# A two-layer decoder trunk: when the second layer's key projection, decays and keys are issued, and where its last scan runs

## The chip, the cores and the metric

The kernel runs on one core of a Trainium2 chip. The metric is the device time of one execution in microseconds. TensorE (PE) multiplies, VectorE (DVE) and ScalarE (ACT) do elementwise work and empty PSUM, GpSimd (POOL) does small copies, and SyncE (SP) issues most DMAs. Each engine works through its own queue in order and waits on semaphores.

## The reference

The input x is 512 tokens by 2048 channels. Each of the two layers computes x <- x + W_out(mixer(RMSNorm(x)) * silu(gate)), in float32. The first layer is differential attention with 8 heads. The second, in which most of the change lies, is RWKV-7 time mixing with 32 heads of 64 channels:

```python
p = h @ w_in                                   # 2048 -> r, k, v, g (2048 each) and two low-rank parts
p = p + (token_shift(p) - p) * mu
r, k, v, g, dw, da = jnp.split(p, RW_SPLITS, axis=-1)
w_log = -softplus(-(w0 + tanh(dw) @ decay_up)) - 0.5
decay = exp(-exp(w_log))
a = sigmoid(a0 + da @ iclr_up)
kk = heads(k * k_k); kk = kk / max(norm(kk), 1e-12)
k = k * (1 + (a - 1) * k_a)
# per head and token: S <- S*decay + (S a_t) b_t + v_t k_t ;  y = S r_t   (a_t = -kk, b_t = kk*a)
y = group_norm(y) * gn_w + gn_b + sum(r*k*r_k) * v
out = (y * silu(g)) @ w_out
```

## The kernel before, in words

**Matmuls.** Every large product is made of three matmuls: operands are split into a high and a low half (ACT rounds, L96 and L592; DVE subtracts, L97 and L593), and `mm3` (L106) sums high·high, high·low and low·high in PSUM. One `unit_chan` (L597) is a projection of 128 channels over 512 tokens: 16 input chunks times three matmuls of 128x512, 48 in all. `unit_tok` (L145) makes 512 output columns of 512 tokens, in four token blocks: 192 matmuls. Weights come from DRAM through SP's queue (L78) into a ring of three buffers (`wraw`, 512 KB in layer 1) and are split part by part.

**The second layer.** `layer1` (L1024) walks over 16 pairs of heads (128 channels each). For pair j it projects keys K, receptances R and values V, and from pair 3 on the gate G of pair j-3 (`LAG`): the order is K R V G. Each projection is emptied by `shift_mix` (L623 on ACT, L624 on DVE: the token shift). `stage1` (L707) takes the keys and two small products of the low-rank parts and makes, on ACT and DVE:

- the decays: tanh (L719), the scan along time (L724), half of the chunk's total (L727), the subtraction (L729), exponentials (L730 to L732);
- the queries: f (L740, L743), AR (L738), l·k (L744);
- the keys: BK (L742 on ACT, L745 on DVE), the squares of the keys and their split (L747, L592, L593), and gam (L734, L735).

`stage2` (L753) puts the receptances into AR (L757) and r (L758). Behind the 18th matmul of the value projection follow `gram` (L762: all products inside the 8 chunks of 64 tokens) and `t_solve` (L814: a triangular solve in some 60 short DVE steps, L834 and L836, then L837; the result goes through DRAM by SP's queue, `td` L838 and `TT` L850, back into SBUF and is transposed on DVE, L858). `stage_v`, L881, makes the values.

**The scan.** While pair j is projected, pair j-1 goes through its 8 chunks one after another. `scan_pair` (L930) is a generator: per chunk the matmul L941 on the state VS, a copy to rhs on ACT (L944), L952 with the solved T, copies on ACT (L954), L959 and the state's update on DVE (L963 twice, L966 in chunk 0). Ahead of it `t_combine` (L844) finishes the inverse with small matmuls (L864, L874). Each `yield` gives a number of matmuls to let pass: `mm3` calls `tick` (L134) after each matmul of a projection, which counts down and issues the chain's next step behind that matmul (`issue_after`). So the order on TensorE is a comb: some matmuls of a projection, one step of the scan, and so on. `chain` (L921) takes the delay before the first step and the two gaps; they are 6 and 8 for pairs with j from 3 to 14, else 4 and 5, and 3 and 4 for the last. `others` hangs further work on a chunk: the transposes of keys (L809) on chunks 0 and 1, of values (L899) on chunk 2, and `finish_y` (L1015, with L1019 and L1021) of pair j-2 on chunk 3.

**What sets the order.** The instructions are issued under priorities: a scan step has offset `SCAN` (3000), other marked parts 2000 or 4000; those ahead in priority are placed earlier in an engine's queue. The queues are in order once built.

**Outputs.** `outputs` (L974), `centre` (L989), `group_norm` (L1001, on the tile `thg` for its squares, L1006) and `finish_y` make a pair's y. `gate` (L906) empties the gate projection, makes the tanh (L910), L911 and the product with y (L912), and stores the row to DRAM, from which `split_rows` loads it for the output projection; the last two rows stay on the chip (`split_row`, L398). After the 16 pairs the gates of pairs 13 to 15 and the last scan follow, and then the output projection in four `unit_tok` blocks, with the residual added and the result stored.

**The first layer** ends in the same way with `unit_tok`; there `all_rows` lets the last attention chain finish behind the output projection's first matmuls, by the parameter `more`.

Of the kernel before, what the change touches and what calls it, by code (L numbers as in the profile page):

```python
# [23 lines left out]
P = 128  # L24
# [89 lines left out]
class Chain:  # L114
# [30 lines left out]
def unit_tok(g, aH, aL, parts, cols, npp=NT, more=None):  # L145

    nc = g.nc
    pts = [g.pp.tile([P, 512], F32, name="pp", tag="pp") if t < npp else
           g.ps.tile([P, 512], F32, name="pt", tag="pb", bufs=2) for t in range(NT)]
    KG = 1024 // cols  # L150
    m = None
    for k0 in range(0, KT, KG):
        raw, fine = g.first.pop(0) if g.first else (None, False)
        wh, wl = split_w(g, parts, KG, cols, k0, raw, fine)
        order = [(k, t) for k in range(KG) for t in range(NT)] if fine else \
                [(k, t) for t in range(NT) for k in range(KG)]
        for i, (k, t) in enumerate(order):
            if more and i in (0, 2, 4):
                more(k0 + (k + 1 + i % 4 // 2 if fine else KG + i // 2), m)
# [267 lines left out]
def layer0(g, aps):  # L427
# [71 lines left out]
    with ExitStack() as cx:  # L499
# [24 lines left out]
        ch = Chain(g, attention(g, h, *before, 17, rows), 4)  # L524

        def all_rows(n, _):
            if n >= KT:
                ch.finish(g)

        yH, yL = Rows(rows, 0), Rows(rows, 1)  # L530
# [175 lines left out]

def stage1(g, j, k, up):  # L707

    nc, w = g.nc, g.work
    p = Pair()  # L710
    col = lambda n: g.prm[n][:, j : j + 1]
    ch = lambda ap: ap.rearrange("p (c t) -> p c t", c=NC_)
    th = []
    for i, nm in enumerate(("hw0", "ha0")):
        (uH, uL), (xH, xL) = up, g.dwda[i]
        ps = g.ps.tile([P, 512], F32, name="pt", tag="pb", bufs=2)
        mm3(nc, ps[:], uH[:, i, :], uL[:, i, :], xH[:], xL[:], True, True)
# [6 lines left out]
    nc.vector.tensor_tensor_scan(l[:].rearrange("p c t -> p (c t)"), g.rmask[:].rearrange("p c t -> p (c t)"),  # L724
                                 lw[:], 0.0, ALU.mult, ALU.add)
    m = g.small.tile([P, NC_], F32, name="m", tag="m")
    nc.vector.tensor_scalar(m[:], l[:, :, C - 1], 0.5, None, ALU.mult)  # L727
    E = w.tile([P, NC_, C + 1], F32, name="E", tag="E", bufs=1)
    nc.vector.tensor_sub(l[:], l[:], m[:, :, None].to_broadcast([P, NC_, C]))  # L729
    nc.scalar.activation(E[:, :, 0], m[:], AF.Exp, scale=-1.0)  # L730
    nc.scalar.activation(E[:, :, 1:], l[:], AF.Exp)
    nc.scalar.activation(l[:], l[:], AF.Exp, scale=-1.0)  # L732
    p.gam = g.small.tile([P, NC_], F32, name="gam", tag="gam")
    nc.vector.tensor_add(p.gam[:, 0 : NC_ - 1], m[:, 0 : NC_ - 1], m[:, 1:NC_])  # L734
    nc.scalar.activation(p.gam[:, 0 : NC_ - 1], p.gam[:, 0 : NC_ - 1], AF.Exp)  # L735
    p.AR = w.tile([P, NC_, 2, C], F32, name="AR", tag="AR", bufs=3)
    BK = w.tile([P, NC_, 2, C], F32, name="BK", tag="BK", bufs=1)
    nc.vector.scalar_tensor_tensor(p.AR[:, :, 0, :], ch(k[:]), col("nkk"), E[:, :, 0:C], ALU.mult, ALU.mult)  # L738
    f = w.tile([P, T], F32, name="f", tag="f", bufs=1)
    nc.scalar.activation(f[:], tha[:], AF.Identity, bias=col("omka"), scale=col("hka"))  # L740
    for i in range(2):
        nc.scalar.activation(BK[:, :, i, :], ch(tha[:]), AF.Identity, bias=col(f"bk_b{i}"), scale=col(f"bk_s{i}"))  # L742
    nc.vector.tensor_mul(f[:], f[:], k[:])  # L743
    nc.vector.tensor_mul(l[:], ch(k[:]), l[:])  # L744
    nc.vector.tensor_mul(BK[:], BK[:], l[:, :, None, :].to_broadcast([P, NC_, 2, C]))  # L745
    k2 = w.tile([P, T], F32, name="k2", tag="thg", bufs=1)
    nc.scalar.activation(k2[:], k[:], AF.Square, scale=col("kk"))  # L747
    p.k2 = split_act(g, k2[:], w, "x")
    p.BK, p.E, p.f = BK, E, f
# [156 lines left out]
def gate(g, j, p, gps, last=False):  # L906
# [5 lines left out]
    nc.vector.tensor_mul(gt[:], gt[:], p.y[:])  # L912
    if last:
        return split_row(g, gt[:])
    nc.scalar.dma_start(out=g.yd2[j * P : (j + 1) * P, :], in_=gt[:])


HEADS = ((0, slice(0, C)), (1, slice(C, P)))
# [11 lines left out]
def scan_pair(g, j, p, gap, gap_s, others):  # L930
# [8 lines left out]
    for c in range(NC_):  # L939
# [20 lines left out]
        for h, r_ in HEADS:  # L960
            s_ = sm[r_, o + h * C : o + h * C + C]
            if c:
                nc.vector.scalar_tensor_tensor(VS[r_, c + 1, h, :], s_, p.gam[r_, c : c + 1], Sg[r_, :],  # L963
                                               ALU.mult, ALU.add)
            else:
                nc.vector.tensor_scalar(VS[r_, c + 1, h, :], s_, p.gam[r_, c : c + 1], None, ALU.mult)  # L966
        if c in others:
# [56 lines left out]
def layer1(g, aps):  # L1024
    nc, tc = g.nc, g.tc
    with ExitStack() as cx:
# [3 lines left out]
        w = g.work  # L1030
        win = aps["rw_w_in"][0]
        pairs = []
        for j in range(D // P):
# [6 lines left out]
            def proj(i, j=j, **k):  # L1040
                return unit_chan(g, [(win, i * D + j * P, P)], P, **k)[0]

            p = stage1(g, j, shift_mix(g, proj(1), P, *mus(g, 1, j), "k", 1), up)
            r = shift_mix(g, proj(0), P, *mus(g, 0, j), "r", 1)
            pairs.append(p)
# [18 lines left out]
            vps = proj(2, behind=(18, behind))  # L1064
            stage_v(g, j, p, vps)
# [7 lines left out]
        for i in range(KT - LAG, KT - 2):  # L1073
            gate(g, i, pairs[i], proj(3, i))
        group_norm(g, j - 1, pairs[j - 1])
        finish_y(g, j - 1, pairs[j - 1])
        gps = [proj(3, i) for i in (j - 1, j)]
        rows = split_rows(g, g.yd2, ("r", "k", "th0", "th1"), 1, j - 1)
        rows.append(gate(g, j - 1, pairs[j - 1], gps[0], True))
        group_norm(g, j, p)  # L1080
        finish_y(g, j, p)
        rows.append(gate(g, j, p, gps[1], True))
        yH, yL = zip(*rows)
# [11 lines left out]
def body(ctx, tc, nc, aps):  # L1095
    g = Ctx()
    g.nc, g.tc = nc, tc
    g.last, g.first = None, []
    g.chains = []
# [39 lines left out]
```

## Time and profile before

| what | us |
|---|---|
| time before, median of 3 runs (lowest to highest) | 2250.93 (2249.58 to 2254.34) |
| the profiled execution | 2247.89 |
| its span on the core | 2246.1 |
| PE busy / PEld busy | 2185.2 / 1767.5 |
| DVE / ACT / POOL busy | 1382.1 / 1006.9 / 285.5 |

The first layer takes about the first 1035 us of the span; the sixteen pairs run from there to about 2040, and the output projection fills the rest. The profile's rows are read so: start and duration in us, engine, line, operation, output tile <- inputs, shape; in brackets the idle time ahead of an instruction and what ended it. In the rows of stretches stand the busy time and count of PE, PEld (weight loads), DVE, ACT and POOL, then the granted clock of TensorE (1.00 is full speed), the DMA share and GB/s. A row of the waits names the waiting engine and line, the one waited for, and the total in us, the times and the longest. The matmul durations in the rows are pipelined latencies; their spacing is what TensorE pays.

### The profile page before, as it was taken

The page shows a single profiled execution, that of the slowest core. Times are in us where ns is not written, and L with a number is a line of the kernel's source. Part 1 is how long each engine was busy: PE and PEld are TensorE (multiplying, and loading weights), DVE is VectorE, ACT ScalarE, POOL GpSimd, SP SyncE. Part 2 cuts the span into 40 slices and gives each one's busy share as a digit, 9 for nine tenths or more (in the row PEclk, how much of TensorE's full clock was granted, in tenths as well). Part 3 has the DMA queues.
Part 4 walks back from the last instruction along what each step waited for, and adds up shares of the span by engine and source line. Part 5 has one row for each costly group of instructions (what it writes and reads, how often), then busy time and mean ns, then how long its engine had stood idle before and what let it go on. Part 6 is the DMA issues. An engine that isn't in the chain of part 4 may idle for free. (4 is left out here: it accounts for less than half of the span.)

```text
span 2246.1 us, 33754 instructions
## 1 busy us (share of the span) xinstructions
PE 2185.2 (97%) x12260; PEld 1767.5 (79%) x12260; DVE 1382.1 (62%) x3666; ACT 1006.9 (45%) x2065; POOL 285.5 (13%) x672
## 2 busy tenths in 40 slices
PE   8999999999999999989899999999999999999999
PEld 6888888888888878877777777787777777777887
DVE  5555646455564663345677787777767787776322
ACT  4443434344343452225465555555555555555221
POOL 0000000000000000000332123232222222231000
PEclk9999999999999999999999999999999999999999
DMA  6222222232223263323422333333333333334433
GB/s 179 94 86 95 85 94 94 85 95 84 95 85 103 86 207 120 131 86 87 106 67 76 79 88 88 94 90 83 92 90 80 82 93 87 97 97 132 141 131 112
DMA packets 290730, 224.46 MB, mean 100 GB/s; under 512 B 47732, under 2 KB 255748, under 8 KB 290564
## 3 DMA queue, kind: packets, MB, share of 16 engines
q1 hardware_dynamic: 275892, 195.74, 30.0%
q0 software_dynamic: 6144, 10.84, 2.0%
q10 hardware_dynamic: 8528, 15.73, 1.9%
q8 instruction: 96, 1.57, 0.3%
q14 instruction: 70, 0.57, 0.1%
HBM read 202.26 MB, written 19.99 MB: 99 GB/s over the span
## 5 line engine op out<-in xcount | busy, mean ns | idle before, releaser
L97 DVE TENSOR_TENSOR wl<-wraw,wh 128x1024 fp32r<-128x1024 f32 (+2 forms) x325 | 395.6, 1217 | 492.8 <-ACT wh L96 488.1
L96 ACT CAST wh<-wraw 128x1024 fp32r<-128x1024 f32 (+2 forms) x325 | 340.2, 1047 | 699.8 <-PE pp L108 468.0
L108 PE MATMUL pp<-wh,hH 128*128 128x512 f32 x1408 | 554.2, 394 | 6.1 <-ACT hH L581 5.8
L108 PE MATMUL pp<-wh,hL 128*128 128x512 f32 x1408 | 552.6, 393 | 0.2 <-DVE hL L582 0.2
L108 PE MATMUL pp<-wl,hH 128*128 128x512 f32 x1408 | 552.3, 392 | 0.0
L108 PE MATMUL pp<-hL,wh 128*128 128x512 f32 (+1 forms) x1056 | 430.3, 407 | 0.1
L108 PE MATMUL pp<-hH,wl 128*128 128x512 f32 (+1 forms) x1056 | 428.8, 406 | 0.0
L108 PE MATMUL pp<-hH,wh 128*128 128x512 f32 (+1 forms) x1056 | 425.2, 403 | 2.1 <-DVE mixt L624 1.8
L108 PEld LDWEIGHTS pp<-wh,hH 128*128 128x128 f32 x1408 | 265.1, 188 | 60.2 <-ACT hH L581 6.5
L108 PEld LDWEIGHTS pp<-wh,hL 128*128 128x128 f32 x1408 | 265.1, 188 | 55.0 <-DVE hL L582 1.5
L108 PEld LDWEIGHTS pp<-wl,hH 128*128 128x128 f32 x1408 | 265.2, 188 | 52.6 <-DVE wl L97 0.3
L108 PEld LDWEIGHTS pp<-hH,wh 128*128 128x128 f32 (+1 forms) x1056 | 199.2, 189 | 40.6 <-DVE mixt L624 2.2
L108 PEld LDWEIGHTS pp<-hL,wh 128*128 128x128 f32 (+1 forms) x1056 | 199.5, 189 | 37.3 <-DVE hL L582 1.7
L108 PEld LDWEIGHTS pp<-hH,wl 128*128 128x128 f32 (+1 forms) x1056 | 199.6, 189 | 33.2
L834 DVE SCALAR_TENSOR_TENSOR tmpl<-LT,Tm 128x60 f32<-128x60 f32 (+24 forms) x496 | 133.2, 269 | 12.6
L947 POOL COPY SA<-VS 64x64 f32<-64x64 f32 x224 | 59.2, 264 | 445.3 <-DVE VS L963 402.5
L836 DVE TENSOR_TENSOR Tm<-Tm,tmpl 128x60 f32<-128x60 f32 (+24 forms) x496 | 105.1, 212 | 11.5 <-DVE tmpl L834 0.4
L673 POOL MEMSET rmask<- 128x512 bf16 x1 | 0.5, 524 | 833.7 <-DVE nb L334 833.7
L963 DVE SCALAR_TENSOR_TENSOR VS<-sm,gam,Sg 64x64 f32<-64x64 f32 x192 | 54.3, 283 | 52.7 <-PE sm L959 48.6
L944 ACT COPY rhs<-sm 64x64 f32<-64x64 f32 x256 | 52.5, 205 | 72.8 <-PE sm L941 70.1
L941 PEld LDWEIGHTS sm<-VS,G 128*128 128x128 f32 x256 | 43.4, 188 | 43.1 <-issue 29.5
L954 ACT COPY VS<-sm 64x64 f32<-64x64 f32 x256 | 52.6, 206 | 53.4 <-PE sm L952 48.7
(269 smaller groups left out, 2813.2 us busy)
## 6 DMA issues: line engine op xcount, KB each, us to landing
wraw<-in_rw_w_in_dram SPq DMA_DIRECT2D x128, 512.0 KB, 4.0
wraw<-in_da_w_in_dram SPq DMA_DIRECT2D x254, 256.0 KB, 3.0
wraw<-in_da_w_out_dram SPq DMA_DIRECT2D x32, 512.0 KB, 3.6
wraw<-in_rw_w_out_dram SPq DMA_DIRECT2D x32, 512.0 KB, 3.6
LT<-ltd POOLq DMA_DIRECT2D x64, 132.0 KB, 2.9
yr<-yd SPq DMA_DIRECT2D x28, 256.0 KB, 3.9
xq<-in_x_dram SPq DMA_DIRECT2D x16, 256.0 KB, 4.9
xd<-xq ACTq DMA_DIRECT2D x16, 256.0 KB, 3.4
```

What stands on the lines that cost most here:

```text
L96: nc.scalar.copy(hi[:, ks], raw[:, ks])
L97: nc.vector.tensor_sub(lo[:, ks], raw[:, ks], hi[:, ks].bitcast(F32))
L108: m = nc.tensor.matmul(out, a, b, start=s, stop=e)
L673: nc.gpsimd.memset(g.rmask[:], 1.0)
L834: nc.vector.scalar_tensor_tensor(tt, LT[:, i : i + 1, i + 1 :].to_broadcast([P, s, n]), n2[:, i : i + 1], Tm[:, 0:s, i : i + 1].to_broadca ...
L836: nc.vector.tensor_add(Tm[:, 0:s, i + 1 :], Tm[:, 0:s, i + 1 :], tt)
L941: nc.tensor.matmul(sm[:, 0:P], both(p.G[:, c, 0]), both(VS[:, c]), start=True, stop=True)
L944: nc.scalar.copy(rhs[r_, :], sm[r_, h * C : h * C + C])
L947: nc.gpsimd.tensor_copy(p.SA[r_, c - 1, :], VS[r_, c, h, :])
L954: nc.scalar.copy(VS[r_, c, h, :], sm[r_, P : P + C])
L963: nc.vector.scalar_tensor_tensor(VS[r_, c + 1, h, :], s_, p.gam[r_, c : c + 1], Sg[r_, :], ALU.mult, ALU.add)
```

## The change

In the second layer:

- The key projection and `stage1` of pair j+1 are issued before the gate projection of pair j-3, its receptance projection after it. The projections so go V, K of the next pair, G, R of the next pair.
- `stage1` ends behind tanh and the decay's bias. The rest becomes three functions, `decays`, `queries` and `keys`, which are put in a list `g.later`; `Chain.step` takes one from the list behind each scan step that has issued a state update (L963 of after's `scan_pair` notes it in `g.state`), with `issue_after` on that update. `stage2` issues what is left. L734 and L735 (gam) go to the end of `keys`; f (L740) goes to the decays, BK's L742 to the queries.
- `gate` is cut in two: `gate` makes gt with the tanh, `gated` the product with y and the store.
- The gaps of the scan of pair 0 are 3 and 4, it begins 28 matmuls later, and the gram of pair 1 no longer issues a step of pair 0's chain right behind itself (`before`).
- The last pair's chain has delay 80 and gaps 4 and 4. It is finished inside the output projection's first block, by `all_rows`, when the last input chunk comes up; then its group norm, `finish_y` and `gated` follow. The gate of pair 15 is projected and its tanh made before.
- `unit_tok`, in both layers, goes chunk by chunk (k outside, token block inside) in the last part of a block if it was given `more`; in the first layer the last row is awaited at `n >= KT - 1` instead of `KT`.

The diff, cut to its core:

```diff
 class Chain:
     def step(self, g):
         with g.tc.high_priority(offset=SCAN):
             self.wait = next(self.steps, None)
+        if g.state and g.later:
+            with g.tc.issue_after(g.state.ins):
+                g.later.pop(0)()
+        g.state = None
...
 def unit_tok(...):
-        order = [(k, t) for k in range(KG) for t in range(NT)] if fine else \
+        by_k = fine or more and k0 + KG == KT
+        order = [(k, t) for k in range(KG) for t in range(NT)] if by_k else \
...
 def stage1(g, j, k, up):
+    def decays():
+        nc.vector.tensor_tensor_scan(l...)            # L724
+        nc.vector.tensor_scalar(m...)                 # L727
+        nc.vector.tensor_sub(l...)                    # L729
+        nc.scalar.activation(p.E[:, :, 0]...); nc.scalar.activation(p.E[:, :, 1:]...)
+        nc.scalar.activation(l...)
+        nc.scalar.activation(p.f...)
+    def queries():
+        nc.vector.tensor_mul(p.f...)                  # L743
+        nc.vector.scalar_tensor_tensor(p.AR...)       # L738
+        nc.vector.tensor_mul(l...)                    # L744
+        for i in range(2):
+            nc.scalar.activation(p.BK[:, :, i, :]...) # L742
+    def keys():
+        nc.vector.tensor_mul(p.BK...)                 # L745
+        nc.scalar.activation(k2...)                   # L747
+        p.k2 = split_act(g, k2[:], w, "x")
+        nc.vector.tensor_add(p.gam...)                # L734
+        nc.scalar.activation(p.gam...)
+    g.later += [decays, queries, keys]
...
 def stage2(g, j, r, p):
+    while g.later:
+        g.later.pop(0)()
...
 def layer1(g, aps):
+        begin(0)
+        r = receptances(0)
         for j in range(D // P):
...
-                chain(g, j - 1, pairs[j - 1], 5, 6 if full else 4, 8 if full else 5, others).step(g)
+                gaps = (6, 8) if full else (4, 5) if j > 1 else (3, 4)
+                chain(g, j - 1, pairs[j - 1], 5, *gaps, others).step(g)
+                if j == 1:
+                    pairs[0].chain.wait += 28
...
-                    gram(g, j, p, j and pairs[j - 1].chain)
+                    gram(g, j, p, j > 1 and pairs[j - 1].chain)
...
+            if j + 1 < D // P:
+                begin(j + 1)
             if j >= LAG:
-                gate(g, j - LAG, pairs[j - LAG], proj(3, j - LAG))
-        chain(g, j, p, 5, 3, 4)
+                gated(g, j - LAG, pairs[j - LAG], gate(g, j - LAG, proj(3, j - LAG)))
+            if j + 1 < D // P:
+                r = receptances(j + 1)
+        chain(g, j, p, 80, 4, 4)
...
+        def all_rows(n, _):
+            if n >= KT and len(rows) < KT:
+                group_norm(g, j, p)
+                finish_y(g, j, p)
+                rows.append(gated(g, j, p, gt, True))
...
-            pts = unit_tok(g, yH, yL, [(aps["rw_w_out"][0], cb * 512, 512)], 512, 2)
+            pts = unit_tok(g, yH, yL, [(aps["rw_w_out"][0], cb * 512, 512)], 512, 2, more=all_rows)
```

More of the change, by code (lines that the diff above doesn't have):

```diff
@@ L158, in unit_tok @@
             if more and i in (0, 2, 4):
-                more(k0 + (k + 1 + i % 4 // 2 if fine else KG + i // 2), m)
+                more(k0 + (k + 1 + i % 4 // 2 if by_k else KG + i // 2), m)
             kk = k0 + k
@@ L526, in all_rows @@
         def all_rows(n, _):
-            if n >= KT:
+            if n >= KT - 1:
                 ch.finish(g)
@@ L738, in stage1 @@
[L738 to L745, printed above, removed]
@@ L903, in turn_values, with gate @@
             nc.scalar.copy(p.VS[(1 - h) * C : (2 - h) * C, par : NC_ : 2, h, :], pv[par * C : par * C + C, :, h, :])
-def gate(g, j, p, gps, last=False):
+def gate(g, j, gps):
     nc, w = g.nc, g.work
@@ L911, in gate, with gated @@
     nc.vector.scalar_tensor_tensor(gt[:], th[:], 1.0, gt[:], ALU.add, ALU.mult)
-    nc.vector.tensor_mul(gt[:], gt[:], p.y[:])
+    return gt
+def gated(g, j, p, gt, last=False):
+    g.nc.vector.tensor_mul(gt[:], gt[:], p.y[:])
     if last:
         return split_row(g, gt[:])
-    nc.scalar.dma_start(out=g.yd2[j * P : (j + 1) * P, :], in_=gt[:])
+    g.nc.scalar.dma_start(out=g.yd2[j * P : (j + 1) * P, :], in_=gt[:])
 HEADS = ((0, slice(0, C)), (1, slice(C, P)))
@@ L962, in scan_pair @@
             if c:
-                nc.vector.scalar_tensor_tensor(VS[r_, c + 1, h, :], s_, p.gam[r_, c : c + 1], Sg[r_, :],
-                                               ALU.mult, ALU.add)
+                g.state = nc.vector.scalar_tensor_tensor(VS[r_, c + 1, h, :], s_, p.gam[r_, c : c + 1], Sg[r_, :],
+                                                         ALU.mult, ALU.add)
             else:
@@ L1032, in layer1, with proj, begin @@
         pairs = []
-        for j in range(D // P):
+        def proj(i, j, **k):
+            return unit_chan(g, [(win, i * D + j * P, P)], P, **k)[0]
+        def begin(j):
             c0 = j * P
@@ L1038, in layer1, with receptances @@
             up = split_act(g, u[:], w, "up")
[L1040 to L1045, printed above, removed]
+            pairs.append(stage1(g, j, shift_mix(g, proj(1, j), P, *mus(g, 1, j), "k", 1), up))
+        def receptances(j):
+            return shift_mix(g, proj(0, j), P, *mus(g, 0, j), "r", 1)
+        begin(0)
+        r = receptances(0)
+        for j in range(D // P):
+            p = pairs[j]
             if j:
@@ L1069, in layer1 @@
                 turn_values(g, p)
+            if j + 1 < D // P:
+                begin(j + 1)
             if j >= LAG:
[L1071 to L1074 removed]
+                gated(g, j - LAG, pairs[j - LAG], gate(g, j - LAG, proj(3, j - LAG)))
+            if j + 1 < D // P:
+                r = receptances(j + 1)
+        chain(g, j, p, 80, 4, 4)
+        gated(g, j - 2, pairs[j - 2], gate(g, j - 2, proj(3, j - 2)))
+        gps = proj(3, j - 1)
         group_norm(g, j - 1, pairs[j - 1])
         finish_y(g, j - 1, pairs[j - 1])
[L1077 to L1083, printed above, removed]
+        row = gated(g, j - 1, pairs[j - 1], gate(g, j - 1, gps), True)
+        gt = gate(g, j, proj(3, j))
+        rows = split_rows(g, g.yd2, ("r", "k", "th0", "th1"), 1, j - 1) + [row]
+        def all_rows(n, _):
[3 more added lines that the diff above has]
+                rows.append(gated(g, j, p, gt, True))
+        yH, yL = Rows(rows, 0), Rows(rows, 1)
         for cb in range(4):
             cs = slice(cb * 512, (cb + 1) * 512)
[L1086 removed]
+            pts = unit_tok(g, yH, yL, [(aps["rw_w_out"][0], cb * 512, 512)], 512, 2, more=all_rows)
             for t in range(NT):
@@ L1098, in body @@
     g.last, g.first = None, []
-    g.chains = []
+    g.chains, g.later, g.state = [], [], None
     g.const = ctx.enter_context(tc.tile_pool(name="const", bufs=1))
```

39 lines of the change are left out of this document (22 added, 17 removed).

## The prediction

> **What bounds the kernel now.** I read the page's first table, then the waits of PE, then the order of DVE in front of the wait that recurs. The page:
>
> ```profile
> span 2246.1 us, 33754 instructions
> PE 2185.2 (97%) x12260; PEld 1767.5 (79%) x12260; DVE 1382.1 (62%) x3666; ACT 1006.9 (45%) x2065; POOL 285.5 (13%) x672
> ```
>
> TensorE is the bound, and the change takes no matmul away. All that can be won is time in which TensorE waits or issues late. For layer 1 (1035 us to the end) the waits of PE are, in us in total, times, longest:
>
> ```profile
> PE sm L941 <- DVE VS L963: 14.8, 14, 1.2
> PE px L864 <- DVE T L858: 6.4, 3, 4.4
> PE sm L941 <- DVE VS L966: 2.9, 1, 2.9
> PE sm L952 <- ACT rhs L944: 1.4, 3, 0.8
> ```
>
> The first row is one wait of about 1.17 us in each of twelve pairs. One of them, and a matmul row further on that fixes the true period of a 128x512 matmul (12 in 2.72 us, so 0.227 each; the 0.39 in the rows is a pipelined latency):
>
> ```profile
> 1521.30 0.39 PE L108 MATMUL pp<-hH,wh 128*128 128x512 f32 x1
> 1522.86 0.46 PE L941 MATMUL sm<-VS,G 128*128 128x128 f32 x2 [1.17 <-DVE VS L963]
> 2095.35 2.72 PE pp L108 x12
> 1473.80:1536.50 62.70, 61.27 (x422) 49.30 (x420) 48.27 (x130) 34.85 (x79) 17.32 (x41) 1.00 0.34 89
> ```
>
> The scan's next step was issued 1.56 us after the matmul before it, where 0.227 would do: the wait costs 1.33 us of a 62.70 us pair (last row: the stretch of one pair, with busy PE, PEld, DVE, ACT, POOL). What makes the state late stands in the order of DVE. The state update of chunk 2 ends at 1497.10, and from there to the update of chunk 6 DVE has no idle time:
>
> ```profile
> 1496.81 0.29 DVE L963 SCALAR_TENSOR_TENSOR VS<-sm,gam,Sg 64x64 f32<-64x64 f32 x1
> 1519.25 1.22 DVE L724 TENSOR_TENSOR_SCAN l<-rmask,th 128x512 f32<-128x512 bf16 x1
> 1520.59 0.68 DVE L743 TENSOR_TENSOR f<-f,mixk 128x512 f32<-128x512 f32 x1
> 1521.29 0.68 DVE L729 TENSOR_TENSOR l<-l,m 128x512 f32<-128x512 f32 x1
> 1522.42 0.29 DVE L963 SCALAR_TENSOR_TENSOR VS<-sm,gam,Sg 64x64 f32<-64x64 f32 x1
> ```
>
> The decay scan and two more row-wide operations stand directly ahead of chunk 6's update, which ends at 1522.71; TensorE follows at 1522.86. I call 1497.10 A: before, the four next steps' L941 start at A+6.77, 12.16, 18.95 and 25.75, and without any wait the last would be at A+24.42.
>
> **The change, part by part.**
>
> *Steady pairs.* The order of after's DVE queue puts the decays (L724, L727, L729) behind chunk 3's update, the queries (L743, L738, L744) behind chunk 4's, the keys (L745, L593, L734) behind chunk 5's. DVE stays without a gap, so what counts is the sum in front of chunk 6's update. These enter that stretch (the scan, l and f were in it already):
>
> ```profile
> 1523.03 0.74 DVE L738 SCALAR_TENSOR_TENSOR AR<-mixk,prm_nkk,E 128x512 f32<-128x512 f32 x1
> 1524.23 0.69 DVE L744 TENSOR_TENSOR l<-mixk,l 128x512 f32<-128x512 f32 x1
> 1524.95 1.23 DVE L745 TENSOR_TENSOR BK<-BK,l 128x1024 f32<-128x1024 f32 x1
> 1527.23 0.68 DVE L593 TENSOR_TENSOR sLx<-k,sHx 128x512 fp32r<-128x512 f32 x1
> ```
>
> With starts 0.08 us before the end shown for the operation in front, and 0.13 for L734, that is +3.1 us. Behind the update go the value mixes L911 and L912 (0.6 each, -1.2) and nine small steps of the triangular solve (L834, L836; -2.2 at their present spacing). That alone is only -0.3. The rest is spacing:
>
> ```profile
> 1510.23 1.22 DVE L97 TENSOR_TENSOR wl<-wraw,wh 128x1024 fp32r<-128x1024 f32 x1
> 1511.37 0.23 DVE L836 TENSOR_TENSOR Tm<-Tm,tmpl 128x70 f32<-128x70 f32 x1
> 1513.11 0.23 DVE L836 TENSOR_TENSOR Tm<-Tm,tmpl 128x66 f32<-128x66 f32 x1
> 1513.37 0.28 DVE L834 SCALAR_TENSOR_TENSOR tmpl<-LT,Tm 128x60 f32<-128x60 f32 x1
> ```
>
> An independent neighbour starts 0.08 us before the end shown (10.23 + 1.22 against 11.37), a dependent one 0.03 us after it (13.11 + 0.23 against 13.37). In after's order some eight more of the solve's steps have an independent operation between them, 0.11 each: -0.9. So chunk 6's update ends at about A+24.5, not 25.6. Going through the steps the same way, L941 comes at A+8.2, 13.8, 19.5 and 24.75, with two waits of about 0.4 left: a gain of 1.0 per pair. At most it is 1.33, at least 0 (all of it lost to the next point). I charge 0.1 for a second limit: ACT now has the casts, tanh, decay, f and both BK activations ahead of chunk 4's rhs copies, in one run. The nearest row, of the 62.7 us from 1485.8:
>
> ```profile
> L742 ACT ACTIVATE BK<-th,prm_bk_b,prm_bk_s 128x512 f32<-128x512 f32 x2 | 1.6, 812 | 0.0
> ```
>
> If both stand uncovered ahead of the copies this is 1.6 us; I count the copies 0.3 late, in a step where DVE is late by more. Twelve waits are shown, the first belongs to the start-up: 11 x 0.9 = **-10 us** (bounds -14.6 and +3.3, that is 1.33 won or 0.3 net lost per pair).
>
> The solve pays for it: its last step moves from A+27.2 to about A+29.7. What follows it:
>
> ```profile
> 1523.89 0.43 DVE L837 TENSOR_TENSOR Tm<-Tm,LT 128x256 f32<-128x256 f32 x1
> 1524.39 0.37 SPq L838 DMA_DIRECT2D td<-Tm  x1
> 1530.31 0.44 DVE L858 STREAM_TRANSPOSE T<-TT 64x256 f32<-64x256 f32 x1
> 1535.50 1.09 PE L864 MATMUL px<-T,G 32*32 32x32 f32 x32
> ```
>
> From the end of L837 to the second L858 pass 6.0 us, and L864 then waits 4.8 us in the queue for its turn (A+38.4). In after the data are there at A+35.7 and L864's turn is at A+37.4. In DVE's order L858 now stands around the eviction of the receptance projection and L757, which puts the second L858's end at about A+37.4 too: cover just enough. SP's queue is moved as well: td now stands behind two weight loads, the second of which needs a buffer that comes free at about A+29.4. I charge nothing; if the cover is gone, the wait is at L864 (rival 2).
>
> *Start-up (pairs 0 to 3).* The scan of pair 0 has few matmuls between its steps. Two successive starts, and the stretch from chunk 1 to chunk 4 (PE, PEld, DVE, ACT, POOL, then clock):
>
> ```profile
> 1132.31 0.46 PE L941 MATMUL sm<-VS,G 128*128 128x128 f32 x2
> 1135.87 0.46 PE L941 MATMUL sm<-VS,G 128*128 128x128 f32 x2
> 1128.70:1139.39 10.69, 10.22 (x47) 6.37 (x46) 8.31 (x32) 5.21 (x18) 3.60 (x10) 1.00 0.20 51
> 1226.75 0.69 PE L864 MATMUL px<-T,G 32*32 32x32 f32 x16 [1.69 <-DVE T L858]
> 1227.60:1231.00 3.40, 3.40 (x23) 2.36 (x22) 1.89 (x4) 1.50 (x3) 3.35 (x4) 0.50 0.58 164
> 1271.70:1275.10 3.40, 3.35 (x16) 2.62 (x16) 3.33 (x8) 3.27 (x9) 0.24 (x1) 1.00 0.24 38
> 1678.10:1681.50 3.40, 3.40 (x10) 2.75 (x10) 3.20 (x8) 1.29 (x2) 0.99 (x4) 0.50 0.37 109
> ```
>
> A step takes 3.56 us. Of the 47 matmuls in three steps 29 are full-width, 29 x 0.227 = 6.6, and 18 are the scan's at some 0.1: 8.4 of 10.69 us, so 0.75 us is lost per step, the round through ACT, PE and DVE. In after's order the scan of pair 0 starts 26 matmuls later behind the gram, has ten to twelve instead of nine matmuls per step and ends six matmuls ahead of the next gram instead of thirty. Each added matmul fills 0.227 us: with two to three more per step, 0.5 x 7 steps = 3.5, and 0.9 off the 4.4 us wait for T (four matmuls' worth more cover): -4.5. The gram of pair 1 no longer issues a step of that chain right behind itself; the number of matmuls stays the same. For pair 1 the same filling (some 2 us) is lost again, as its T solve has less cover and its L864 waits about 1.3 longer: 0. For pair 2, the wait of 1.69 us is followed by 3.4 us at a granted clock of 0.50, which costs 1.7; both go if its solve, started some 4 us earlier, is in time: -3.4. The 1.17 wait at 1271 shrinks by 0.5. Together **-8.5 us**; bounds -12 and -2, since none of these rows shows the new order. What tells when a wait costs double is the clock column: 0.50 behind 1.69 us, 1.00 behind 1.18 us.
>
> [...]
>
> *Tail.* The last scan now runs inside the first block of the output projection, not beside the last two gate projections:
>
> ```profile
> 2042.58:2074.17 31.59, 30.09 (x153) 20.55 (x154) 18.94 (x35) 19.34 (x53) 10.63 (x20) 1.00 0.54 167
> PE sm L952 <- ACT rhs L944: 0.8, 1, 0.8
> PE pt L1019 <- DVE yc L1012: 0.6, 1, 0.6
> ```
>
> 153 matmuls in 31.59 us: 78 full-width (17.7 us) and 75 of the scan, some 8.3 with their switching, leave 5.6 us lost, the 0.8 wait among it; the 0.6 at L1019 stands just before. With gaps of 4 for 3 and the scan over about 100 matmuls I take two thirds back, 3.9, and the 0.6: **-4.5 us** (bounds -6 and -2). The row that this scan gives is first needed for the last input chunk, now the 180th of 192 matmuls since the last part goes chunk by chunk (by_k); its transposes (L1019) come as the 156th, 24 x 0.227 = 5.4 us ahead, against some 3.5 us for L1021, L912 and the two halves of split_row. Evictions of the four blocks end within the last twelve matmuls instead of spread out; four additions of 0.7 us fit.
>
> *Layer 0.* by_k in its last part and a later finish of its last attention chain change no matmul and no count; what ends there last, TensorE's wait for the norm, stays: 0, within 0.3.
>
> **Sum.** -8.5 - 10 - 4.5 = -23. The profiled execution took 2247.89 us (span 2246.1 and 1.8 around it), so 2224.9; the median of the runs shown is 2250.93, 3.0 above it. I forecast that median: **2228 us**.
>
> **Rivals.**
>
> *1. The steady gain does not come (about 2237).* DVE has no idle time from chunk 2 to chunk 6 either way; without the spacing gain the sum falls by 0.3 only, and if ACT is late as well the wait moves to chunks 4 and 5. Then only start-up and tail pay: 2250.9 - 13 = 2238, less a little. For it: ACT's long run in front of the copies. Against it: the two spacings in the rows. [...] The rows show a start before the shown end for independent neighbours, and so speak for a gain.
>
> *2. Slower (about 2270): T comes too late in each pair.* Place: SP's queue, td behind two weight loads, and L858, with L757 queued behind it on DVE and the gram behind that. One load in the way:
>
> ```profile
> wraw<-in_rw_w_in_dram SPq DMA_DIRECT2D x128, 512.0 KB, 4.0
> ```
>
> T then lands up to 4 us later, L864 waits 2 to 3 us, and above 1.69 us of idle the half clock adds 1.7: about 4 a pair, 3 net of the gain, 11 x 3 = +33 against the other -13: +20. It decides from 1.7 us of delay on, as there is no slack beyond A+37.4. Against it: the buffer that the load waits for comes free before the solve's end, and issuing takes 0.4 us, not 4.
>
> *3. Nothing net (about 2250).* Small waits at L864 (0.3 to 0.9 per pair) and ACT's lateness use up the 0.9 per pair, and the start-up's tighter solves bring half clocks of their own that cost what its scans win.
>
> **Chances.** Forecast 0.56 (own range 2219 to 2234), rival 1 0.20, rival 3 0.10, rival 2 0.14. All lower bounds together, -12 - 14.6 - 6 = -32.6, give 2218; all upper ones, -2 + 3.3 - 2, give 2250. Range 2217 to 2252, which leaves out rival 2 and a little. 0.2% is 4.5 us, about what a measurement of this kernel can tell from no change: faster 0.76, same 0.10, slower 0.14.
>
> **What would show it.** In the changed profile: waits of L941 for L963 in the steady pairs two of about 0.4 us or none, a pair of 61.7 to 61.9 us between grams, no wait of L864 for T beyond pair 2, and no clock of 0.50 after 1300 us but for the single 2.9 us wait at L966 (the clock row at 1678; a one-off, in no sum). The gram of pair 2 about 4.5 us earlier; the scan in the output projection with steps of 3.5 us or more and no wait at L1019. The forecast is wrong if L864 shows a wait in each pair, if L952 waits for ACT's copies in each pair, or if the solve's late end pushes DVE's work past the gram.

## The result and the profile after

The changed kernel takes **2236.76 us** (median of 4 runs, 2235.41 to 2238.46) against 2250.26 us (4 runs, 2249.11 to 2254.34). The ratio is 0.9937, with a 95% interval of 0.992 to 0.9954: faster by 13.5 us. I had forecast 2228 us, 23 us faster, in a range from 2217 to 2252 (2219 to 2234 for the forecast proper).

The first lines of the page of the changed kernel:

```profile
span 2233.7 us, 33774 instructions
PE 2184.1 (98%) x12260; PEld 1770.4 (79%) x12260; DVE 1374.9 (62%) x3666; ACT 1005.1 (45%) x2065; POOL 297.4 (13%) x672
```

The span is 12.4 us shorter and TensorE's busy time nearly the same: only waiting went. The starts of the sixteen grams (the first L773 of before, L789 of after) cut both traces into stretches with the same matmuls, so the difference can be located (one profile of each kernel):

| stretch | before, us | after, us | measured | forecast |
|---|---|---|---|---|
| start to gram of pair 1 | 1102.45 | 1102.19 | -0.3 | 0 |
| pair 1 to pair 2 | 60.03 | 61.30 | +1.3 | -4.5 |
| pair 2 to pair 4 | 122.92 | 117.96 | -5.0 | -4.0 |
| pair 4 to pair 15 (eleven pairs) | 694.73 | 691.32 | -3.4 | -10 |
| pair 15 to the end | 265.97 | 260.93 | -5.0 | -4.5 |

Two stretches fell short, the eleven steady pairs and the one from pair 1 to pair 2. The waits of PE in the eleven pairs of after:

```profile
PE px L880 <- DVE T L874: 3.7, 8, 0.8
PE sm L961 <- DVE VS L986: 2.9, 1, 2.9
PE sm L979 <- ACT VS L974: 2.5, 11, 0.2
PE sm L961 <- DVE VS L983: 2.0, 11, 0.2
PE gp L789 <- DVE AR L773: 0.8, 1, 0.8
```

The wait of 1.17 us for the state is gone from each pair; a fifth of a microsecond is left in two places. In the first row stands what took its place: L880 (L864 of before) waits for T in some of the pairs; before has no such wait in these eleven. The lone 2.9 us came back at the same pair, so it is no one-off, as I had called it; it belongs to both kernels.

In a pair that lost nothing, DVE's order in after, from chunk 2's update (first row) to chunk 6's (last but one), and TensorE's step behind it:

```profile
1489.91 0.29 DVE L983 SCALAR_TENSOR_TENSOR VS<-sm,gam,Sg 64x64 f32<-64x64 f32 x1
1499.89 1.22 DVE L738 TENSOR_TENSOR_SCAN l<-rmask,th 128x512 f32<-128x512 bf16 x1
1503.90 0.29 DVE L983 SCALAR_TENSOR_TENSOR VS<-sm,gam,Sg 64x64 f32<-64x64 f32 x1
1506.58 0.74 DVE L749 SCALAR_TENSOR_TENSOR AR<-mixk,prm_nkk,E 128x512 f32<-128x512 f32 x1
1509.61 0.29 DVE L983 SCALAR_TENSOR_TENSOR VS<-sm,gam,Sg 64x64 f32<-64x64 f32 x1
1510.06 1.28 DVE L756 TENSOR_TENSOR BK<-BK,l 128x1024 f32<-128x1024 f32 x1
1514.98 0.29 DVE L983 SCALAR_TENSOR_TENSOR VS<-sm,gam,Sg 64x64 f32<-64x64 f32 x1
1515.43 0.46 PE L961 MATMUL sm<-VS,G 128*128 128x128 f32 x2
```

The scan, AR and BK each have an update behind them, and L961 follows chunk 6's update without a wait. Half of what the pair wins stands elsewhere, though, where no wait was shown. The scan's first matmul on rhs in a pair, in before and in after:

```profile
1481.05 0.43 PE L952 MATMUL sm<-rhs,TT 128*128 128x64 f32 x2
1474.42 0.33 PE L972 MATMUL sm<-rhs,TT 128*128 128x64 f32 x2
```

The full-width matmul ahead of the first row starts at 1480.51, 0.54 us earlier; the one ahead of the second at 1474.18, 0.24 us earlier. With a like 0.17 us at the next chunk, chunk 2's update comes 22.7 us behind the gram instead of 23.3. Now the pair that ends at 1592.41: first SP's queue with two weight loads, then td and TT; then DVE and TensorE.

```profile
1579.21 3.38 SPq L78 DMA_DIRECT2D wraw<-in_rw_w_in_dram  x2
1582.68 0.53 SPq L854 DMA_DIRECT2D td<-Tm  x1
1588.48 1.82 SPq L866 DMA_DIRECT2D TT<-td  x4
```

```profile
1590.23 0.44 DVE L874 STREAM_TRANSPOSE T<-TT 64x256 f32<-64x256 f32 x1 [1.61 <-DMA TT<-td]
```

```profile
1590.73 0.69 PE L880 MATMUL px<-T,G 32*32 32x32 f32 x16 [0.81 <-DVE T L874]
1591.80 0.69 PE L880 MATMUL px<-T,G 32*32 32x32 f32 x16 [0.39 <-DVE T L874]
```

The TT loads wait for td to land, 5.8 us after its issue; in before 1524.39 to 1526.73, 2.3 us, was usual (eight of the eleven pairs; 2.9 to 4.0 in the others). In after td takes 4.2 to 5.8 us in ten of them, in the clean pair too. The second load of the first row is issued at 1582.2, half a microsecond ahead of td. DVE stood idle for 1.6 us for the data, and TensorE 0.8 and 0.4 us behind it (the second since L773 stands between the two transposes on DVE). Stretches of a clean pair, of this one, and of the gram that follows it (the third column from the right is the granted clock):

```profile
1467.49:1529.16 61.67, 61.19 (x424) 49.31 (x421) 47.60 (x131) 34.47 (x79) 18.57 (x41) 1.00 0.35 90
1529.16:1592.41 63.25, 61.54 (x423) 49.33 (x420) 47.66 (x131) 34.91 (x79) 18.57 (x41) 1.00 0.35 88
1592.40:1595.80 3.40, 3.40 (x35) 3.39 (x32) 0.13 (x1) 2.42 (x5) 0.00 (x0) 0.51 0.40 119
```

The clean pair takes 61.67 us, 1.04 less than before, as forecast. The late one takes 63.25, and the gram behind it runs at half clock for 3.4 us, which costs the next pair 1.7 more (63.40 us). Behind a like wait, 0.82 and 0.44 us at 1784, the clock stayed at 1.00.

### The profile page after: what moved, and what is told of

It is laid out like the page before. It is cut to its first block, busy times and chain, and to the rows that moved or that the text cites. A ratio compares the mean times of both kernels' runs of the same rounds, so it can differ in the third digit from the quotient of the medians.

```text
span 2233.7 us, 33774 instructions
## 1 busy us (share of the span) xinstructions
PE 2184.1 (98%) x12260; PEld 1770.4 (79%) x12260; DVE 1374.9 (62%) x3666; ACT 1005.1 (45%) x2065; POOL 297.4 (13%) x672
## 5 line engine op out<-in xcount | busy, mean ns | idle before, releaser
L970 POOL TENSOR_SCALAR Sg<-SA,gam 128x64 f32<-128x64 f32 x96 | 72.1, 751 | 9.3
```

Of the source, the lines that this page charges most:

```text
L970: nc.gpsimd.tensor_scalar(Sg[:], p.SA[:, c - 1, :], p.gam[:, c : c + 1], None, ALU.mult)
```

## The experiments

Theory: in the steady pairs the load on SP right ahead of td makes T late; the gain of 1.0 us per pair is there and is given back at L880. Rivals: T is late because the solve ends 2.5 us later on DVE, whatever SP does; or the gain itself is missing in part.

**The load behind TT.** Only the second half of the key weights moves, from pair 4 on. They are loaded two pairs ahead, so the edit acts on T of pair 2 and of those after it.

```diff
+        after = g.last or k0 and g.hold
-        with g.tc.issue_after(g.last) if g.last else ExitStack():
+        with g.tc.issue_after(after) if after else ExitStack():
             ld = g.nc.sync.dma_start(...)
...
+    g.tdq = m.ins                    # the last TT load
...
+            g.hold = g.tdq if j > 3 else None
+            ps = proj(1, j)
+            g.hold = None
```

> The changed kernel with one edit: from pair 4 on, the second half of the key projection's weights (512 KB) is issued on SP behind the four TT loads instead of right ahead of td. Theory (the load in front of td on SP's queue delays T): TT's issue comes 2.3 to 3 us after the solve's end instead of 4.4 to 6.0, no wait of L880 for T in the steady pairs, no clock of 0.5 at their grams, all steady pairs at 61.7 to 61.9 us; 7 us less, 2229 to 2231 us. Rival A (T is late because the solve ends later, the load is harmless): TT's issue stays at 4.4 us or more, 2236 to 2238 us. Rival B (the load is only put off and comes too late for its own cast): waits of L108 for wl, 2237 us or more.

Measured: 2230.2 us (2225.68 to 2231.67), ratio to before 0.9916 (0.9901 to 0.9931). SP's queue at the pair that ends at 1528.99, and its L882 (L880 of after):

```profile
1520.72 0.38 SPq L855 DMA_DIRECT2D td<-Tm  x1
1523.06 1.82 SPq L867 DMA_DIRECT2D TT<-td  x4
1524.93 1.85 SPq L79 DMA_DIRECT2D wraw<-in_rw_w_in_dram  x2
```

```profile
1527.97 1.09 PE L882 MATMUL px<-T,G 32*32 32x32 f32 x32
```

td lands in 2.3 us again, the load comes behind TT, and L882 has no wait. The waits of PE in its eleven pairs hold no row for T any more:

```profile
PE sm L963 <- DVE VS L988: 2.8, 1, 2.8
PE sm L981 <- ACT VS L976: 2.6, 12, 0.2
PE sm L963 <- DVE VS L985: 1.9, 11, 0.2
```

Over the pairs TT's issue comes 2.4 to 3.5 us after the solve's end (after: 4.4 to 6.0, and 3.1 in the last), all but the long pair take 61.5 to 62.1 us, and the eleven pairs 685.6 us, 9.1 less than before and 5.7 less than after. The solve ends as late as in after (53.1 to 53.5 us behind the gram in the ordinary pairs of both). So the load was the cause, and the rival with the solve's end falls.

**The load between td and TT.** The same edit, with td in place of the last TT load (`g.prev` is td of the pair whose T is on its way).

```diff
+    g.tdq = nc.sync.dma_start(out=g.td[...], in_=Tm[:]).ins
...
+            g.hold = g.prev if j > 3 else None
```

> The changed kernel with the same load issued between td and the TT loads. If the order in the queue decides (td is served after what was issued ahead of it), td lands in about 2.4 us again, but the TT loads now come behind the 512 KB: their landing takes 3 to 4 us instead of 1.8, and the sum of both is 1 to 2 us better than in the changed kernel: 2231 to 2235 us. If the transfers only share the engines, whatever their order, td still takes 4 us or more: 2236 to 2238 us.

Measured: 2239.09 us (2237.45 to 2241.06), ratio 0.9959 (0.9945 to 0.9973): not faster than after (the intervals overlap), against the first reading. SP's queue at one pair, the landing of its TT loads, and the waits for T in all of layer 1 (in after 7.1 us, 12 times):

```profile
1780.29 0.38 SPq L855 DMA_DIRECT2D td<-Tm  x1
1780.76 0.53 SPq L79 DMA_DIRECT2D wraw<-in_rw_w_in_dram  x1
1782.83 2.10 SPq L867 DMA_DIRECT2D TT<-td  x4
```

```profile
DMA to landing us min/median/max: 2.4/3.4/3.6
```

```profile
PE px L881 <- DVE T L875: 8.4, 9, 2.8
```

This is the worst of the steady pairs. Over the ten that the edit reaches, td, now ahead of the load, lands in 2.3 to 3.6 us instead of 4.2 to 5.8, and the slowest of the TT loads behind it in 2.0 to 3.6 us instead of 1.9 to 2.2. The eleven pairs take 688.1 us, 3.2 less than in after and 2.5 more than with the load behind TT. So in this run the order decides, and there the first reading held. The total did not follow, for a place that neither reading had looked at, the solve of pair 2, where two weight loads come between td and TT:

```profile
1221.86 1.12 SPq L79 DMA_DIRECT2D wraw<-in_rw_w_in_dram  x2
1229.32 0.69 PE L881 MATMUL px<-T,G 32*32 32x32 f32 x16 [2.43 <-DVE T L875]
1230.80:1241.04 10.24, 10.24 (x68) 7.85 (x67) 5.56 (x17) 5.05 (x12) 2.15 (x5) 0.50 0.40 106
```

The TT loads land there in 4.7 to 5.0 us instead of 2.0 to 2.3, L881 waits 2.4 us instead of 0.7, and half clock follows for 10.2 us (last row) where after has none: pair 3 to pair 4 takes 70.4 us instead of 65.4. Another 2.6 us of this profile stand ahead of the gram of pair 1, where the edit has no part. In these runs, then, what is issued shortly behind a 512 KB load lands late (td in 4.2 to 5.8 us instead of 2.3, TT in up to 3.6 instead of 2.2), and the load costs least behind the whole round trip (685.6 us for the eleven pairs, against 688.1 and 691.3).

**The parts at once.**

```diff
-    g.later += [decays, queries, keys]
+    for part in decays, queries, keys:
+        part()
```

> The changed kernel with decays, queries and keys issued at once at the end of stage 1 instead of in parts behind three state updates. Theory (the parts win, since the 3.1 us of queries and keys otherwise stand ahead of chunk 4's update, with waits of DVE for ACT's exponentials between them): L961 waits 1.5 to 4 us in each steady pair, half clock behind it where it is above 1.7 us; pairs of 63.5 to 66 us, 2255 to 2285 us. Rival (the key projection ahead of the gate does it alone): pairs as in the changed kernel, 2235 to 2239 us.

Measured: 2242.44 us (2238.77 to 2243.48), ratio 0.997 (0.996 to 0.998). Six of its eleven steady pairs take 62.6 to 62.7 us, the others 61.6 to 64.2 and the long one 66.8: between the two expectations, and for another reason than mine. The waits of PE from 1470 to 1660 us hold one row, and none for the state:

```profile
PE sm L980 <- ACT VS L975: 0.7, 3, 0.2
```

The wait for the state is gone without the parts (in all eleven pairs but the long one): with the keys emptied right behind chunk 3, the queue's own order already has the scan ahead of chunk 4's update and AR and BK ahead of chunk 5's. That pairs are no shorter comes from elsewhere: the two halves of L881 now stand around and inside the gram.

```profile
1659.32 0.69 PE L881 MATMUL px<-T,G 32*32 32x32 f32 x16
1659.93 0.48 PE L790 MATMUL gp<-AR,BK 64*128 64x128 f32 x2
1660.35 0.69 PE L881 MATMUL px<-T,G 32*32 32x32 f32 x16
```

Adding up the starts on TensorE, L881, gram and L891 take 0.5 to 0.7 us longer in such a pair than in after's clean pair and the scan's steps 0.4. So the key projection's place removes the wait, but no time: the eleven pairs take 695.0 us, against 694.7 in before and 691.3 in after. The 1.0 us per pair came only with the parts in their fixed places, and not for my reason: without them L881 and the scan's steps lose as much as the wait cost.

**The start-up as before.**

```diff
-                gaps = (6, 8) if full else (4, 5) if j > 1 else (3, 4)
+                gaps = (6, 8) if full else (4, 5)
-                if j == 1:
-                    pairs[0].chain.wait += 28
-                    gram(g, j, p, j > 1 and pairs[j - 1].chain)
+                    gram(g, j, p, j and pairs[j - 1].chain)
```

> The changed kernel without its start-up edits: pair 0's gaps are 4 and 5, no 28 matmuls of delay, the gram of pair 1 issues a step of its chain. Theory (the edits lose 1.3 us between the grams of pairs 1 and 2 by a longer stretch at half clock, and win 2.5 us in each of the next two): 60 us between grams 1 and 2, 55 and 67 us in the next two; 3 to 4 us more, 2240 to 2241 us. Rival (the 2.5 us of the two later stretches come from the order of the projections and the parts, not from these edits): 60, 52.6 and 65.4 us; 1 us less, 2235 to 2236 us.

Measured: 2240.06 us (2232.98 to 2246.82), ratio 0.9958 (0.9942 to 0.9974). Its runs spread over 14 us, so the total does not tell it from after; the one profile does, stretch by stretch. Pair 1 to 2 takes 61.05 us, 2 to 3 54.22, 3 to 4 66.52. The three stretches sum to 181.8 us against 179.3 in after and 183.0 in before. So the edits bring 2.8 us behind pair 2, and the rest there, 2.2, comes from the rest of the change. That the edits lengthen the first stretch, as I had it, is not so: it hardly changes without them, though half clock lasted some 7 us here and 10 in after.

**Both kernels, profiled a second time.**

> The kernel before, unchanged, profiled a second time: what repeats between two profiles. If the length of the half clock behind pair 0's wait belongs to the kernel, it is again 3.4 us, and grams 1 to 2 are 60.0 us apart; if it belongs to the moment at which the wait falls, it may be 3.4 or 6.8 us and the stretch differs by up to 2 us. td to TT 2.3 to 4.1 us and steady pairs of 62.7 us either way, and the long pair of 67 us at 1662 again.

> The changed kernel, unchanged, profiled a second time. Theory: TT's issue again 4.4 to 6.0 us after the solve's end in every steady pair, and the sum of the eleven pairs within 2 us of 691.3, though the pairs that lose need not be the same ones, since T misses L880's turn by tenths of a microsecond. If the losses belonged to certain pairs, the same ones lose again. Half clock behind pair 0's wait again about 10 us.

Measured: 2249.39 and 2235.85 us. First the stretch from pair 1 to pair 2 in before, its repeat, after and its repeat:

```profile
1102.45:1162.48 60.03, 54.80 (x369) 40.35 (x369) 43.07 (x129) 30.24 (x73) 19.13 (x41) 0.97 0.29 71
```

```profile
1102.72:1162.99 60.27, 55.38 (x368) 40.75 (x368) 43.04 (x129) 30.31 (x73) 18.80 (x41) 0.94 0.28 72
```

```profile
1102.19:1163.49 61.30, 57.69 (x369) 42.45 (x369) 44.19 (x132) 30.72 (x73) 18.95 (x41) 0.92 0.31 77
```

```profile
1105.33:1165.39 60.06, 56.13 (x368) 41.36 (x369) 44.14 (x132) 30.76 (x73) 18.98 (x41) 0.94 0.32 78
```

The clock's mean of 0.97, 0.94, 0.92 and 0.94 says 3.4, 6.8, 10.2 and 6.8 us at half speed: (1 - 0.94) x 60 / 0.5 is about 7. The time at half speed is here one, two or three pieces of 3.4 us, and not the same in two profiles of one kernel. With equal clocks (the two repeats) the stretch is 60.27 against 60.06: the change wins 0.2 us there, one profile each. The +1.3 of the first comparison so goes with the clock, though a piece has no fixed price here: one more cost before 0.24 us (60.03 to 60.27) and after 1.24 (60.06 to 61.30). The kernel with the old start-up, also at some 7 us, took 61.05: read so, the edits win 1.0 us, and the rest of the change costs 0.8. In the first profiles of both kernels the stretches at half clock begin whole numbers of 3.413 us apart, in before at 1118.3, 1227.6 and 1678.1 (32 and 132 such pieces) and in after at 1118.0, 1592.4 and 1670.9 (139 and 23). So where a wait falls on this grid of 3.413 us may matter, an estimate of mine from two places in after: both waits at 1592 lie in the piece from 1589.0 to 1592.4, with 1.20 us of idle, and half clock follows; at 1784, with the clock at 1.00 behind it, a border at 1783.6 (56 pieces behind 1592.4) parts the idle into 0.45 and 0.81. The idle in a piece alone does not decide: 1.06 us, all in the piece that begins at 1101.3, was not enough in before, while waits of 0.37 and 0.36 us were in after's repeat (below).

In before again the steady pairs take 62.7 us and the long one 66.9. In after's repeat TT's issue came 4.3 to 5.9 us after the solve's end (2.8 in the last pair), and the eleven pairs take 689.2 us, 2.2 less than in the first profile. Four pairs lost in both: those that end at 1407, 1594, 1658 and 1787 us took 62.5, 63.3, 64.2 and 63.2 (1405, 1592, 1656 and 1786 us in the first: 62.4, 63.3, 63.4, 63.2). Two more lost in the first only, those that end at 1910 and 1973 (62.7 each; 61.6 and 62.0 in the repeat). What singles the four out stays open. Half clock came again behind the waits at 1592 (0.79 and 0.36 us here), and here also behind 0.37 and 0.36 us at 1658, for 6.8 us.

**Pair 0's scan 50 matmuls later,** on the kernel with the load behind TT.

```diff
-                gaps = (6, 8) if full else (4, 5) if j > 1 else (3, 4)
+                gaps = (6, 8) if full else (4, 5) if j > 1 else (2, 3)
-                    pairs[0].chain.wait += 28
+                    pairs[0].chain.wait += 50
```

> The kernel with the key load behind TT, and pair 0's scan 50 instead of 28 matmuls later with gaps of 2 and 3: L880 of pair 0 then stands behind 52 instead of 42 matmuls. Theory (the 2.3 us wait and the 10 us of half clock behind it cost 2.3 + 5 us between grams 1 and 2, the scan's shorter gaps 2 to 3): no wait above 1 us, no half clock, grams 1 to 2 at 55.5 to 57 us, total 2225 to 2227 us. Rival (the clock falls for another reason, or the scan with 2 and 3 matmuls between its steps loses as much): 60 us or more, 2229 to 2232 us.

Measured: 2232.45 us (2231.21 to 2234.41), ratio 0.9921 (0.9906 to 0.9936); pair 1 to 2 takes 60.38 us. This did not test the theory, as the edit made a wait of its own:

```profile
PE px L882 <- DVE y L906: 4.6, 1, 4.6
```

So late in the order, the tile of L882's products shares its PSUM buffer with the one from which L906 makes y, and has to wait for it.

**The end as before.**

```diff
-        chain(g, j, p, 80, 4, 4)
+        chain(g, j, p, 5, 3, 4)
...
-            pts = unit_tok(..., 512, 2, more=all_rows)
+            pts = unit_tok(..., 512, 2)
```

(with group norm, `finish_y` and `gated` of the last pair ahead of the output projection again)

> The changed kernel with the end of before: the last pair's chain with delay 5 and gaps 3 and 4 beside the last two gate projections, its row made before the output projection, no chunk-by-chunk order there. Theory (the scan's place is worth what the traces differ by, 5.1 us): 266 us from the last gram to the end instead of 260.9, total 2241 to 2243 us. Rival (the end is shorter for another reason, for instance since gates and loads no longer meet): 261 to 263 us, 2236 to 2239 us.

Measured: 2240.66 us (2236.74 to 2243.37), ratio 0.9953 (0.994 to 0.9966). From the last gram to the end it takes 265.79 us, against 260.93 in after and 265.97 in before, and the two waits of before are back:

```profile
PE sm L972 <- ACT rhs L964: 0.9, 1, 0.9
PE pt L1039 <- DVE yc L1032: 0.6, 1, 0.6
```

The scan's place is worth 4.9 us; only the total came a little under the expected one.

**One comparison on one chip.** The changed kernel, the load behind TT from pair 4 on, and from pair 2 on (`if j > 1`).

> The changed kernel again, on one chip with the next two, so that the edit's worth is read from one comparison. About 0.6% under before, 2235 to 2238 us; the pairs that end at 1405, 1592, 1656 and 1786 us lose again.

> The kernel with the key load behind TT again, in five rounds. Theory: about 7 us under the changed kernel on the same chip, 2228 to 2231 us, 0.85 to 0.95% under before, with an interval that does not reach the changed kernel's ratio. If the first comparison was luck of the chip, within 3 us of the changed kernel.

> The same edit for the pairs 2 and 3 as well, which moves a few instructions of the start-up. If T's lateness costs there too (0.7 us of wait at pair 2), 1 us less than the version with pair 4 on; if the start-up is bound by its clock and its scan, no difference, and up to 2 us more where the scan's place moves.

Measured against one before of 2249.01 us: 2234.86 us (ratio 0.9935, 0.9923 to 0.9947), 2231.03 us (0.9918, 0.9905 to 0.9931) and **2227.8 us** (0.9911, 0.9896 to 0.9925). The edit is worth 3.8 us there between the medians. The interval of the second does reach the first kernel's ratio, against what I expected; the traces carry the verdict: 692.0 us for the eleven pairs, 684.2 and 684.5, some of it the clock's, as half clock took 10.2 us of these pairs in the first, none in the second and 3.4 in the third. Over all the profiles taken, after needs 691.3, 689.2 and 692.0 us for them and the kernels with the load behind TT 685.6, 685.8, 684.2 and 684.5: some 6 us less on average. In after's profile here the pairs that end at 1406, 1592, 1658 and 1787 lost again (62.5, 63.3, 65.7, 62.4). The third version is 3.2 us below the second, but their intervals overlap. Its profile gains 2.3 us, nearly all in the first stretch (58.62 us from pair 1 to 2 against 60.91). There the edit also moves a load that stood between td and TT of pair 0: the wait for T is 1.7 us instead of 2.2, and half clock lasts 6.8 us instead of 10.2. After's repeat, with as much half clock, took 60.06.

## Why the prediction was right, and where it was short

- **The number: in the wide range, outside the narrow one.** 2236.76 us lies within 2217 to 2252, which adds all bounds up, but not within 2219 to 2234, where I had the forecast at 0.56. It lies beside rival 1's 2237, and that is chance: rival 1 let DVE keep the state late, but the state came on time, and most of the gain was lost at T.
- **Steady pairs, the wait removed: right, the size partly by luck.** 62.71 to 61.67 us in a clean pair; I had 1.0 before a charge of 0.1. L961 stands 8.2, 14.1, 19.9 and 25.2 us behind chunk 2's update, 0.0 to 0.5 later than I had it. So from there the last step comes only 0.5 us earlier than before (25.75), not 1.0; the other 0.6 was won ahead of chunk 2's update, where I had counted nothing. The two small waits left are shown as 0.2 and cost 0.4 and 0.3 in spacing, as I had them; but 24.42 without any wait and two of 0.4 make 25.2, so my 24.75 did not follow from my own waits. Without the late T the eleven pairs win 9.1 us (load behind TT); I had 10. That the parts were needed is right for the time and not for the wait: the key projection's place alone removes the wait and wins nothing.
- **"I charge nothing" for T's way: the step that failed.** I let 6.0 us pass from the solve's end to the start of the second L858, as in before (where it is 6.0 to 7.3). Measured: 7.3 to 8.9 us in after, since td's landing took 4.2 to 5.8 us (2.9 in the last pair) instead of 2.3. I had seen the two loads ahead of td in the queue, but counted only the time at which the second is issued, not that td's transfer runs behind its 512 KB. L880 waited in the pairs with 5 us and more, 0.4 to 1.3 us, and half clock added 1.7 behind one of them. That is rival 2, in place and mechanism, at a fraction of its size: of the 11 us that eleven clean pairs would win, 7.6 are missing, 0.7 per pair instead of 4. The waits shown for T (3.7 us), that half clock (1.7) and one wait for AR (0.8, at the last pair) make 6.2 of them; with the load behind TT 5.7 came back.
- **"above 1.69 us of idle the half clock adds": too lax.** Two waits of 0.81 and 0.39 with small matmuls between them were enough (the clock row of 0.51 above), and so were 0.37 and 0.36 in the repeat; 0.82 and 0.44 at another pair were not.
- **Start-up, pair 1 to 2: wrong.** I had -4.5, it is about -0.2 at an equal clock. The wait for T did shrink (4.1 to 2.6 us between the repeats), but the filling did not save the scan's steps: summed over the stretch, the first matmuls of the steps start some 2.8 us later than the spacing of full-width matmuls (0.227 us) would have it, in both repeats. The updates and copies come later too, as DVE and ACT now hold the next pair's keys in that stretch. That last sentence is argued from the order, not tried.
- **Start-up, pair 2 to 4: -5.0, forecast -4.0,** but otherwise divided: -2.5 and -2.5 where I had 0 and -4. Without the start-up edits it is -2.2.
- **Tail: right.** -5.0 against -4.5, and undone by itself +4.9. No wait at L1039, none at the scan.
- **Layer 0: not resolved.** -0.3 in the first profiles, +2.6 in the repeats, where after had half clock for 3.4 us at 1037.8; other profiles of after's start-up lie between.
- **Sum.** -23 forecast, -12.4 measured in the spans and -13.5 in the medians. In the spans 6.6 are missing in the steady pairs and 5.8 in the first stretch; pair 2 to 4, the tail and layer 0 gave 1.8 more.

## What to carry to other kernels

When a change uses up slack, look at what stands ahead of each small transfer in its queue: here a 512 KB load half a microsecond ahead of a 128 KB store added 2 to 3.5 us to its landing, and one edit of the order brought some 6 us in eleven pairs. Such an edit must be followed through every place that it reaches: with the load between td and TT the steady pairs won 3.2 us, and the stretch behind pair 2's solve lost 5, half clock included. That a wait is gone does not mean that its time is won: with the parts issued at once the wait was gone and the pairs took as long as before. And a stretch that ends in a short idle of TensorE should be profiled twice, since the time at half clock was not the same in two profiles here (behind pair 0's wait 3.4 and 6.8 us in before, 10.2 and 6.8 in after).

## What the runs showed of the hardware that I had not expected

- A 128 KB store (td) issued 0.5 us behind a 512 KB load, from the same queue, landed in 4.2 to 5.8 us in after instead of 2.3, the usual time in before; issued ahead of the load, with the load between td and TT, in 2.3 to 3.6. The slowest of the four 32 KB loads (TT) behind such a load took 2.0 to 3.6 us there instead of 1.9 to 2.2, and 5.0 behind two of them.
- Half clock came behind idles of 0.81 and 0.39 us with sixteen 32x32 matmuls between them in after, at the same pair in its repeat behind 0.79 and 0.36, and there once behind 0.37 and 0.36; behind 0.82 and 0.44 in another pair of after, and behind a single idle of 1.18 us in before (at 1271.7), the clock stayed at 1.00.
- The stretches at half clock begin whole numbers of 3.413 us apart in the first profiles of before and after. The time at half clock behind pair 0's wait for T was 3.4 and 6.8 us in two profiles of before, and 10.2, 6.8 and 10.2 us in three of after.
